# Splitting activation sums into high and low halves in the up projection instead of the down projection

## The chip, the cores and the metric

The kernel runs on one core of a Trainium2 chip. The metric is the device time of one execution in microseconds; the profile shows the same program executed once under the hardware profiler. Every time below is of that one core.

## What is computed

One layer of a hybrid decoder, followed by a final norm. This study touches its MLP alone:

```python
h2 = rmsnorm(x, norm2_g)
act = jnp.square(jax.nn.relu(jnp.einsum('bld,df->blf', h2, w_up)))
return x + jnp.einsum('blf,fd->bld', act, w_down)
```

There are 1024 tokens, a width of 1024 and a hidden width of 4096. All is float32.

## The kernel before

**Split products.** TensorE multiplies in float32r. Each operand is held as a high half and a low half: `split` (L73) casts the source to float32r on ACT (`nc.scalar.copy`, L77) and subtracts that from the source on DVE (L78). Every product is then three matmuls: high by high, high by low, low by high (L99 to L104, L715, L1091).

**Two projections.** The hidden width is cut into 32 rows of 128 (`NF`). The first four (`FS = 4`) are done in the standard way and stored in `act_dram`. The other 28 go in 14 pairs by a Strassen-Winograd scheme of seven products in place of eight.

**The up projection** (L984 to L1012) is a loop over these 14 pairs. In each pair `strassen_run` (L705) issues seven products of 12 matmuls, in the order 1, 5, 6, 2, 7, 3, 4. Products are summed in banks: `al_` takes 1, 6, 7 and 4, `be` takes 5 and 3, `ga` takes 2. Between them `keep_copy` (L718) copies a bank to a `cc` tile on ACT, and `put` (L987) adds bank and copy on DVE (L992) and applies ReLU on ACT (L993 or L990) into one half of one of the pair's two `go` tiles. The add after product 7 writes the half that holds a22. The tag `go` has two buffers, so the next pair's `go` tiles are the same two, and a write to them waits until all that reads the old contents is done, the DMAs too. After product 5 `up_load` loads the weights of a later pair (`strassen_load`, L683): two DMAs on SP into `raw` tiles of two buffers, sums of weight blocks on POOL (`s12`, L692 and L693; `s34`, L696 and L697), and splits (`hi`/`lo`, `sh`/`sl` twice, `eh`/`el`). The low half of `s34` is read by product 7 and product 3.

When a pair is complete its two tiles are squared (L998), four sums of blocks are made on DVE (L1006 to L1009), and seven blocks are written to `sum_dram` (L1012): a11, a21, a12 and a22 in the `go` tiles, and three in `sums`, a tile of one buffer. Each write is 128x512 float32, 256 KB, in rows of 512 bytes. It is issued from ACT's queue, but for the last pair from SP's.

**The down projection.** First come the four standard rows (L1021 to L1028, L1141 to L1144). Then the 28 rows go in seven groups `c` of two pairs, and each group in four units `m` of 256 tokens. A group's weights are loaded and split by `down_w` (L1044): loads on SP, block differences on POOL, splits on ACT and DVE. A unit's sums are loaded by `down_s` (L1068): one DMA of 896 KB on SP into `s_raw`, which has one buffer, then two splits: the five blocks of the first products into `s_hi` and `wide`, the two blocks of products 7 and 4 into a late tile (`lo` or `s_late`). A unit runs seven products of six matmuls (L1087). Their results are added to `x1` on DVE (L1097 to L1115); one of these adds, L1097, moves the bank `al` to `ga`, and the next product in `al` waits for it. Product 7 and product 4 of a unit are run inside the next unit.

**Order.** The source order is not the order in the queues. The tile framework gives every instruction its place by its own schedule, in which the source order is a priority, and sets the semaphores; each engine then runs its own queue strictly in order. Buffers are reused in turn per tag, and `reserve` (L669) lays out the tags of a pool.

Of the kernel before, what the change touches and what calls it, by code (L numbers as in the profile page):

```python
# [11 lines left out]
F32 = mybir.dt.float32  # L12
F32R = mybir.dt.float32r
# [5 lines left out]
P = 128  # L19
D = 1024  # L20
# [27 lines left out]
def hybrid_trunk_kernel(ctx: ExitStack, tc: tile.TileContext, x_tok, metas, vecs, gains, w_in, w_br, w_pool,  # L48
# [21 lines left out]
    def new(pl, shape, dt, tag, bufs=None):  # L70
        return pl.tile(shape, dt, tag=tag, name=nm(tag), **({} if bufs is None else {"bufs": bufs}))

    def split(hi, lo, src, eng=None, heng=None):  # L73
        if heng:
            heng.tensor_copy(hi, src)
        else:
            nc.scalar.copy(hi, src)  # L77
        (eng or nc.vector).tensor_sub(lo, src, hi.bitcast(F32))  # L78
# [58 lines left out]
    x1_dram = dram.tile([NB, P, D], F32, name="x1_dram")  # L137
    FS = 4
    act_dram = dram.tile([FS, P, T], F32, name="act_dram")
    sum_dram = dram.tile([(NF - FS) // 2, 4, P, 7, P], F32, name="sum_dram")  # L140


    hstack = ctx.enter_context(ExitStack())
# [525 lines left out]
    def reserve(pl, *tags):  # L669
        for tag, n, shape in tags:  # L670
            for _ in range(n):
                new(pl, [P, shape], F32, tag, n)
# [7 lines left out]
            t[w, i] = new(pl, [P, 4, 512], F32R, f"t{w}{i}")  # L680
        return [t["h", i] for i in range(4)], [t["l", i] for i in range(4)]

    def strassen_load(pl, src_a, src_b, eng=nc.gpsimd):  # L683
        ra = new(wst, [P, KD, P], F32, "raw")
        nc.sync.dma_start(ra, src_a)
        rb = new(wst, [P, KD, P], F32, "raw")
        nc.sync.dma_start(rb, src_b)
        ah, al = new(wst, [P, KD, P], F32R, "hi"), new(wst, [P, KD, P], F32R, "lo")
        split(ah, al, ra)
        s12, s34 = new(pl, [P, 2, 4, P], F32, "sf", 2), new(pl, [P, 2, 4, P], F32, "sf", 2)  # L690
        a11, a12, a21, a22 = ra[:, 0:4, :], ra[:, 4:8, :], rb[:, 0:4, :], rb[:, 4:8, :]
        eng.tensor_add(s12[:, 0], a21, a22)  # L692
        eng.tensor_sub(s12[:, 1], s12[:, 0], a11)  # L693
        s12h, s12l = new(pl, [P, 2, 4, P], F32R, "sh", 2), new(pl, [P, 2, 4, P], F32R, "sl", 2)
        split(s12h, s12l, s12)
        eng.tensor_sub(s34[:, 0], a11, a21)  # L696
        eng.tensor_sub(s34[:, 1], a12, s12[:, 1])  # L697
        s34h, s34l = new(pl, [P, 2, 4, P], F32R, "sh", 2), new(pl, [P, 2, 4, P], F32R, "sl", 2)
        split(s34h, s34l, s34)
        eh, el = new(pl, [P, 4, P], F32R, "eh", 2), new(pl, [P, 4, P], F32R, "el", 2)  # L700
        split(eh, el, a22)
        return {1: (ah[:, 0:4], al[:, 0:4]), 2: (ah[:, 4:8], al[:, 4:8]), 3: (s34h[:, 1], s34l[:, 1]), 4: (eh, el),
                5: (s12h[:, 0], s12l[:, 0]), 6: (s12h[:, 1], s12l[:, 1]), 7: (s34h[:, 0], s34l[:, 0])}
# [223 lines left out]
    with ExitStack() as st:  # L927
# [25 lines left out]
                nc.sync.dma_start(t, src)  # L953

        p2 = pool("up", 1, None, st)
        reserve(p2, ("go", 2, T), *STRASSEN_TAGS[1:])

        def up_load(f):
            if f < NF:
                return strassen_load(p2, w_up[f], w_up[f + 1], nc.gpsimd if f > FS + 2 else nc.vector)  # L960

        X1A = 4

# [20 lines left out]
        for f in range(FS, NF, 2):  # L984
            outs = [new(p2, [P, T], F32, "go", 2) for _ in range(2)]

            def put(r, c, ps, add):  # L987
                dst = outs[r][:, c * 512:(c + 1) * 512]
                if add is None:
                    nc.scalar.activation(dst, ps, AF.Relu)  # L990
                else:
                    nc.vector.tensor_add(dst, ps, add)  # L992
                    nc.scalar.activation(dst, dst, AF.Relu)  # L993

            lhs = strassen_run(p2, lhs, h2_hi, h2_lo, th, tl, put, lambda: up_load(f + 2),
                               first_rows if f + 2 == NF else None)
            for t in outs:
                nc.scalar.activation(t, t, AF.Square)  # L998
            (a11, a21), (a12, a22) = ((t[:, :512], t[:, 512:]) for t in outs)
            sums = new(p2, [P, 3, 512], F32, "sums", 1)  # L1000
            eng = nc.scalar
            if f + 2 == NF:
                eng = nc.sync
                x1 = new(dn, [P, NB, D], F32, "x1", 1)
                load_x1(range(X1A))
            nc.vector.tensor_sub(sums[:, 1], a11, a21)  # L1006
            nc.vector.tensor_add(a21, a21, a22)
            nc.vector.tensor_sub(sums[:, 0], a21, a11)
            nc.vector.tensor_sub(sums[:, 2], a12, sums[:, 0])  # L1009
            dst = sum_dram[(f - FS) // 2].rearrange("m p i t -> p i m t")  # L1010
            for i, t in enumerate((a11, a21, a12, sums[:, 0], sums[:, 2], sums[:, 1], a22)):
                eng.dma_start(dst[:, i], t.rearrange("p (m t) -> p m t", m=4))  # L1012

        load_x1(range(X1A, NB))
        st.close()
# [50 lines left out]
            return h, l  # L1066

        def down_s(c, m):  # L1068
            raw = new(dn, [P, 2 * D], F32, "s_raw", 1)[:, :14 * P].rearrange("p (u j) -> p u j", u=2)
            nc.sync.dma_start(raw, sum_dram[2 * c:2 * c + 2, m].rearrange("u p i t -> p u (i t)"))  # L1070
            h, l = new(dw, [P, 2, 5 * P], F32R, "s_hi", 2), new(dn, [P, 2 * D], F32R, "wide")
            l = l[:, :10 * P].rearrange("p (u t) -> p u t", u=2)
            split(h, l, raw[:, :, :5 * P])
            late = new(wst, [P, D], F32R, "lo") if (4 * c + m) % 3 else new(dn, [P, D], F32R, "s_late", 1)
            late = late.rearrange("p (v u t) -> p v u t", v=2, u=2)
            split(late[:, 0], late[:, 1], raw[:, :, 5 * P:])
            return (h, l), (late[:, 0], late[:, 1])

        class Unit:
            def __init__(self, tw, c, m):  # L1080
                self.tw, self.s, self.m = tw, down_s(c, m), m
                self.al, self.be, self.ga = (bank(t) for t in ("mm", "z", "tr"))

            def acc(self, r, c):
# [75 lines left out]
        prev, last = None, NU // 2 - 1  # L1160
        for c in range(NU // 2):
            tw = [down_w(2 * c), down_w(2 * c + 1)]
            if c == last:
                fg = new(wst, [P, D], F32, "hi")
                nc.sync.dma_start(fg, gains[2])
                wide = [new(dw, [P, 7 * 512], F32, ("wa", "wb")[c % 2]) for _ in range(3)]
                outs = [t[:, i * D:(i + 1) * D] for t in wide for i in range(3)]
            for m in range(4):
                unit = Unit(tw, c, m)
                if c == last and m == 3:  # L1170
                    unit.end(prev)
                    break
                unit.one()
                if prev:
                    prev.two()
                unit.three()
                if c == last:
                    final(m, 1)
                if prev:
                    prev.four()  # L1180
                    if c == last and m:
                        final(prev.m + 4, 0)
                prev = unit
# [60 lines left out]
```

## Time and profile before

| | us |
|---|---|
| Median of the three runs | 1981.67 |
| Their range | 1977.3 to 1984.02 |
| The profiled execution, its own time | 1980.0 |
| Its span, first to last instruction | 1978.2 |
| PE busy in the span | 1931.9 |
| DVE busy | 1291.9 |
| ACT busy | 844.0 |
| POOL busy | 329.1 |

PE is TensorE's matmul stream, PEld its weight loads, DVE is VectorE, ACT is ScalarE, POOL is GpSimd and SP is SyncE. An issue of a DMA from ACT's or SP's queue is written ACTq or SPq and is not counted as busy, though it takes its place in that queue. A line such as `sl<-sf,sh` names the tile written and the tiles read. Matmuls overlap: each is shown with its whole length, while the next one starts earlier. So PE shows as busy throughout when matmuls follow each other without a gap, and a stall shorter than the overlap is not seen as idle.

### The profile page before, as it was taken

To read this page: it belongs to the slowest core of one execution; us is meant where nothing else is said; L and a number is where in the kernel's file an instruction comes from. 1 tells how busy PE (TensorE), PEld (TensorE's weight loads), DVE (VectorE), ACT (ScalarE), POOL (GpSimd) and SP (SyncE) were. 2 spreads that over 40 slices of the span, in tenths; PEclk is the share of its full clock that TensorE was granted. 3 is DMA by queue.
4 is the path that set the end of the run, shared out by engine and by line. 5 is a ranking of instruction groups with operands and counts; after the bars stand their busy time and mean duration, and the time that the engine had idled before them with its cause. 6 is when DMAs were issued, how large, how long until landed. Compare 5 with 4: busy or idle time off the path is not lost.

```text
span 1978.2 us, 25779 instructions
## 1 busy us (share of the span) xinstructions
PE 1931.9 (98%) x9974; PEld 1647.4 (83%) x9974; DVE 1291.9 (65%) x1783; ACT 844.0 (43%) x1452; POOL 329.1 (17%) x280
## 2 busy tenths in 40 slices
PE   8999999999999999999999999999999999999998
PEld 7889899988899888888887888888888887777876
DVE  6677877666768844344334667479555546888887
ACT  6556654233324433333342112255544544343445
POOL 1000001111000033333320000000323212322322
PEclk9999999999999999999999999999999999999999
DMA  3000101110102233333326554242454557343433
GB/s 140 33 33 22 43 33 49 54 43 26 40 33 91 85 149 117 139 123 112 128 104 231 186 187 169 77 143 93 136 170 138 155 165 258 127 145 135 152 138 137
DMA packets 112076, 224.61 MB, mean 114 GB/s; under 512 B 8129, under 2 KB 58817, under 8 KB 111954
## 3 DMA queue, kind: packets, MB, share of 16 engines
q1 hardware_dynamic: 56706, 175.22, 25.9%
q10 hardware_dynamic: 55248, 47.75, 7.2%
q8 instruction: 78, 1.28, 0.3%
q14 instruction: 44, 0.36, 0.1%
HBM read 157.40 MB, written 65.54 MB: 113 GB/s over the span
## 4 chain that ended last, share of the span: by engine, by line
PE 76%; DVE 9%; issue 9%; DMA 3%; ACT 2%; POOL 1%; POOLq 0%; DVEq 0%; ACTq 0%; SPq 0%
PE mm L715 18%; PE mm L104 9%; PE mm L103 9%; PE mm L102 9%; PE z L715 9%; PE tr L715 5%; PE mm L1092 3%; PE z L1092 2%; PE av L362 1%; PE z L582 1%; DVE wb L78 1%; PE tr L1092 1%; DVE keep L339 1%; DVE wa L78 1%; DMA raw<-in_w_dn_dram 1%
## 5 line engine op out<-in xcount | busy, mean ns | idle before, releaser
L102 PE MATMUL mm<-h_hi,hi 128*128 128x384 f32 (+4 forms) x880 | 303.0, 345 | 1.4 <-DVE a L198 1.0
L103 PE MATMUL mm<-h_lo,hi 128*128 128x384 f32 (+4 forms) x880 | 295.2, 336 | 1.1 <-DVE h_lo L78 1.1
L104 PE MATMUL mm<-h_hi,lo 128*128 128x384 f32 (+4 forms) x880 | 295.8, 336 | 0.0
L103 PEld LDWEIGHTS mm<-h_lo,hi 128*128 128x128 f32 x880 | 166.6, 189 | 7.9 <-DVE h_lo L78 1.9
L104 PEld LDWEIGHTS mm<-h_hi,lo 128*128 128x128 f32 x880 | 166.0, 189 | 8.0
L102 PEld LDWEIGHTS mm<-h_hi,hi 128*128 128x128 f32 x880 | 166.0, 189 | 7.9 <-DVE a L198 1.4
L78 DVE TENSOR_TENSOR sl<-sf,sh 128x1024 fp32r<-128x1024 f32 x68 | 83.8, 1232 | 128.8 <-ACT sh L77 128.8
L692 POOL TENSOR_TENSOR sf<-raw 128x512 f32<-128x512 f32 x30 | 40.3, 1342 | 764.1 <-DMA raw<-in_w_up_dram 459.3
L78 DVE TENSOR_TENSOR lo<-raw,hi 128x1024 fp32r<-128x1024 f32 x76 | 95.7, 1259 | 45.2 <-ACT hi L77 44.8
L77 ACT CAST hi<-raw 128x1024 fp32r<-128x1024 f32 x76 | 79.9, 1052 | 77.0 <-PE mm L103 40.7
L715 PE MATMUL mm<-th,sh 128*128 128x512 f32 x272 | 106.2, 390 | 0.0
L77 ACT CAST sh<-sf 128x1024 fp32r<-128x1024 f32 x68 | 71.4, 1052 | 81.3 <-PE z L715 41.7
L715 PE MATMUL mm<-tl,sh 128*128 128x512 f32 x272 | 105.8, 389 | 0.0
L715 PE MATMUL mm<-th,sl 128*128 128x512 f32 x272 | 105.8, 389 | 0.0
L339 DVE TENSOR_TENSOR_SCAN keep<-keep 128x1040 f32<-128x1040 f32 (+3 forms) x64 | 88.9, 1390 | 25.7 <-ACT keep L332 18.9
L102 PE MATMUL mm<-b_hi,eh 128*128 128x512 f32 x256 | 99.6, 390 | 1.8 <-DVE mixed L884 1.8
L103 PE MATMUL mm<-b_lo,eh 128*128 128x512 f32 x256 | 100.1, 391 | 0.1
L104 PE MATMUL mm<-b_hi,el 128*128 128x512 f32 x256 | 99.6, 390 | 0.5 <-DVE el L78 0.5
L78 DVE TENSOR_TENSOR el<-raw,eh 128x512 fp32r<-128x512 f32 x34 | 36.2, 1064 | 64.5 <-ACT eh L77 61.3
L334 POOL TENSOR_SCALAR_AFFINE_SELECT keep<-keep 128x128 f32<-128x128 f32 x64 | 22.3, 348 | 300.2 <-ACT keep L332 260.2
L77 ACT CAST at_h<-tr 128x384 fp32r<-128x384 f32 (+2 forms) x112 | 54.5, 495 | 36.6 <-PE tr L349 34.9
L77 ACT CAST s_hi<-s_raw 128x1280 fp32r<-128x1280 f32 x28 | 35.4, 1266 | 80.9 <-DMA s_raw<-sum_dram 45.8
(439 smaller groups left out, 5019.2 us busy)
## 6 DMA issues: line engine op xcount, KB each, us to landing
raw<-in_w_in_dram SPq DMA_DIRECT2D x76, 512.0 KB, 3.7
s_raw<-sum_dram SPq DMA_DIRECT2D x28, 896.0 KB, 4.8
gate_dram<-go ACTq DMA_DIRECT2D x32, 512.0 KB, 2.6
go<-gate_dram SPq DMA_DIRECT2D x32, 512.0 KB, 3.7
raw<-in_w_up_dram SPq DMA_DIRECT2D x32, 512.0 KB, 3.8
raw<-in_w_dn_dram SPq DMA_DIRECT2D x29, 512.0 KB, 4.4
sum_dram<-go ACTq DMA_DIRECT2D x52, 256.0 KB, 4.7
sum_dram<-sums ACTq DMA_DIRECT2D x39, 256.0 KB, 4.8
```

The lines of the kernel that those rows point to most:

```text
L77: nc.scalar.copy(hi, src)
L78: (eng or nc.vector).tensor_sub(lo, src, hi.bitcast(F32))
L102: nc.tensor.matmul(ps, lh, rh, start=first, stop=False)
L103: nc.tensor.matmul(ps, lh, rl, start=False, stop=False)
L104: nc.tensor.matmul(ps, ll, rh, start=False, stop=last)
L334: nc.gpsimd.affine_select(out=t[:, :P], in_=t[:, :P], compare_op=ALU.is_gt, fill=1.0, base=0, pattern=[[1, P]], channel_multiplier=-1)
L339: nc.vector.tensor_tensor_scan(t, t, t, 1.0, op0=ALU.mult, op1=ALU.min)
L362: nc.tensor.matmul(av[:, :w], pair.vv[e][:, b, :], a[:, b, :w], start=i == 0 and a is at[0], stop=i == len(order) - 1 and a is at[1])
L582: nc.tensor.matmul(ps[:, c * 64:(c + 1) * 64], xc, low, start=True, stop=True)
L692: eng.tensor_add(s12[:, 0], a21, a22)
L715: nc.tensor.matmul(ps, lhs[i][x][:, k, :], rhs[i][y][:, k, :], start=fresh and k == 0 and n == 0, stop=k == 3 and n == 2, skip_group_check ...
L1092: nc.tensor.matmul(ps, x, y[:, rs], start=fresh and k == 0 and n == 0, stop=k == 1 and n == 2, skip_group_check=not fresh)
```

## The change

Four edits belong together.

- The up projection splits each of the seven blocks before it is written. The high half goes to a new tile `hs` of three buffers; the low half is written over the block itself. Both halves are written to `sum_dram`, which gets one more dimension `v` of two: 14 writes of 256 KB per pair in place of seven.
- The pool `up` reserves a list of tags with `hs` in it, and `strassen_load` in the up projection is called with `inplace=True`: `sf` has one buffer, and `s34` is written over `ra`, the `raw` tile that it is computed from.
- `down_s` loads high and low halves straight into the tiles that the matmuls read, in four DMAs per unit; `s_raw` and both splits go.
- `down_s` of the next unit is called right after a unit is made, one unit ahead of where it stood; `Unit` takes the loaded sums as an argument.

```diff
-    sum_dram = dram.tile([(NF - FS) // 2, 4, P, 7, P], F32, name="sum_dram")
+    sum_dram = dram.tile([(NF - FS) // 2, 4, 2, P, 7, P], F32, name="sum_dram")
...
-    def strassen_load(pl, src_a, src_b, eng=nc.gpsimd):
+    def strassen_load(pl, src_a, src_b, eng=nc.gpsimd, inplace=False):
...
-        s12, s34 = new(pl, [P, 2, 4, P], F32, "sf", 2), new(pl, [P, 2, 4, P], F32, "sf", 2)
+        s12 = new(pl, [P, 2, 4, P], F32, "sf", 1 if inplace else 2)
+        s34 = ra.rearrange("p (i k) c -> p i k c", i=2) if inplace else new(pl, [P, 2, 4, P], F32, "sf", 2)
...
-        reserve(p2, ("go", 2, T), *STRASSEN_TAGS[1:])
+        reserve(p2, ("go", 2, T), ("cc", 3, 512), ("sf", 1, D), *STRASSEN_TAGS[3:], ("hs", 3, 512))
...
-                return strassen_load(p2, w_up[f], w_up[f + 1], nc.gpsimd if f > FS + 2 else nc.vector)
+                return strassen_load(p2, w_up[f], w_up[f + 1], nc.gpsimd if f > FS + 2 else nc.vector, True)
...
-            dst = sum_dram[(f - FS) // 2].rearrange("m p i t -> p i m t")
+            dst = sum_dram[(f - FS) // 2].rearrange("m v p i t -> v p i m t")
             for i, t in enumerate((a11, a21, a12, sums[:, 0], sums[:, 2], sums[:, 1], a22)):
-                eng.dma_start(dst[:, i], t.rearrange("p (m t) -> p m t", m=4))
+                h, l = new(p2, [P, 512], F32R, "hs", 3), t.bitcast(F32R)
+                split(h, l, t)
+                for v, part in enumerate((h, l)):
+                    eng.dma_start(dst[v, :, i], part.bitcast(F32).rearrange("p (m t) -> p m t", m=4))
...
         def down_s(c, m):
-            raw = new(dn, [P, 2 * D], F32, "s_raw", 1)[:, :14 * P].rearrange("p (u j) -> p u j", u=2)
-            nc.sync.dma_start(raw, sum_dram[2 * c:2 * c + 2, m].rearrange("u p i t -> p u (i t)"))
             h, l = new(dw, [P, 2, 5 * P], F32R, "s_hi", 2), new(dn, [P, 2 * D], F32R, "wide")
             l = l[:, :10 * P].rearrange("p (u t) -> p u t", u=2)
-            split(h, l, raw[:, :, :5 * P])
             late = new(wst, [P, D], F32R, "lo") if (4 * c + m) % 3 else new(dn, [P, D], F32R, "s_late", 1)
             late = late.rearrange("p (v u t) -> p v u t", v=2, u=2)
-            split(late[:, 0], late[:, 1], raw[:, :, 5 * P:])
+            for v, main in enumerate((h, l)):
+                src = sum_dram[2 * c:2 * c + 2, m, v].rearrange("u p i t -> p u (i t)")
+                nc.sync.dma_start(main.bitcast(F32), src[:, :, :5 * P])
+                nc.sync.dma_start(late[:, v].bitcast(F32), src[:, :, 5 * P:])
             return (h, l), (late[:, 0], late[:, 1])
...
             tw = [down_w(2 * c), down_w(2 * c + 1)]
+            if not c:
+                s = down_s(0, 0)
...
             for m in range(4):
-                unit = Unit(tw, c, m)
+                unit, s = Unit(tw, s, m), None
+                if 4 * c + m + 1 < 4 * (last + 1):
+                    s = down_s(c + (m + 1) // 4, (m + 1) % 4)
```

More of the change, by code (lines that the diff above doesn't have):

```diff
@@ L1068, in down_s, with __init__ @@
         def down_s(c, m):
-            raw = new(dn, [P, 2 * D], F32, "s_raw", 1)[:, :14 * P].rearrange("p (u j) -> p u j", u=2)
-            nc.sync.dma_start(raw, sum_dram[2 * c:2 * c + 2, m].rearrange("u p i t -> p u (i t)"))
             h, l = new(dw, [P, 2, 5 * P], F32R, "s_hi", 2), new(dn, [P, 2 * D], F32R, "wide")
             l = l[:, :10 * P].rearrange("p (u t) -> p u t", u=2)
-            split(h, l, raw[:, :, :5 * P])
             late = new(wst, [P, D], F32R, "lo") if (4 * c + m) % 3 else new(dn, [P, D], F32R, "s_late", 1)
             late = late.rearrange("p (v u t) -> p v u t", v=2, u=2)
-            split(late[:, 0], late[:, 1], raw[:, :, 5 * P:])
+            for v, main in enumerate((h, l)):
+                src = sum_dram[2 * c:2 * c + 2, m, v].rearrange("u p i t -> p u (i t)")
+                nc.sync.dma_start(main.bitcast(F32), src[:, :, :5 * P])
+                nc.sync.dma_start(late[:, v].bitcast(F32), src[:, :, 5 * P:])
             return (h, l), (late[:, 0], late[:, 1])
         class Unit:
-            def __init__(self, tw, c, m):
-                self.tw, self.s, self.m = tw, down_s(c, m), m
+            def __init__(self, tw, s, m):
+                self.tw, self.s, self.m = tw, s, m
                 self.al, self.be, self.ga = (bank(t) for t in ("mm", "z", "tr"))
```

## The prediction

> **What bounds the kernel now.** I read the page's span first, then the busy time of each engine by stretch, then what TensorE (PE) waits for in the down projection, then one pair of the up projection in order of time. The windows' columns are: stretch, its length, busy time of PE, PEld, DVE, ACT and POOL, granted clock, DMA share, GB/s. The first row is the 14 Strassen pairs of the up projection, the second the turn to the down projection, the third its units up to the last, the fourth the tail, the fifth one pair.
>
> ```profile
> span 1978.2 us, 25779 instructions
> 1374.70:1641.20 266.50, 266.50 (x1177) 220.73 (x1177) 141.36 (x161) 134.89 (x185) 68.26 (x48) 1.00 0.52 151
> 1641.20:1686.50 45.30, 44.21 (x194) 35.91 (x193) 34.70 (x43) 15.81 (x19) 16.89 (x11) 1.00 0.68 245
> 1686.50:1955.50 269.00, 259.85 (x1124) 210.51 (x1123) 228.51 (x296) 115.09 (x161) 71.93 (x49) 0.99 0.42 144
> 1955.50:1978.20 22.70, 13.20 (x56) 9.92 (x54) 16.14 (x40) 11.23 (x29) 5.86 (x5) 0.89 0.31 116
> 1489.00:1508.05 19.05, 19.05 (x86) 15.78 (x85) 9.96 (x12) 9.54 (x13) 5.59 (x5) 1.00 0.54 153
> ```
>
> PE is busy without a gap in the up projection, so nothing can be gained there; work added to ACT or DVE is free only while PE never waits for it. In the units of the down projection PE is idle 269.00 - 259.85 = 9.15 us, and DVE is busy 228.51/269 = 85%: that is the only place where this change can gain. What PE waits for there (total, times, longest):
>
> ```profile
> PE mm L1092 <- DVE tr L1097: 7.7, 7, 2.3
> PE mm L1092 <- DVE wide L78: 1.3, 3, 0.5
> ```
>
> The second is the low half of the sums itself; the first is an add that stands in DVE's queue behind splits, those of the sums among them. One pair of the up projection, ACT's queue, then DVE's and PE's (start, length, engine):
>
> ```profile
> 1488.99 0.37 ACTq L1012 DMA_DIRECT2D sum_dram<-go  x1
> 1489.41 0.60 ACT L990 ACTIVATE go<-mm 128x512 f32<-128x512 f32 x1 [0.44 <-PE mm L715]
> 1490.96 1.06 ACT L998 ACTIVATE go<-go 128x1024 f32<-128x1024 f32 x1 [0.96 <-DVE sums L1006]
> 1491.93 0.56 ACT L720 COPY cc<-mm 128x512 f32<-128x512 f32 x1
> 1492.06 1.09 ACTq L1012 DMA_DIRECT2D sum_dram<-go  x2
> 1493.51 1.46 ACTq L1012 DMA_DIRECT2D sum_dram<-sums  x2
> 1495.01 1.50 ACTq L1012 DMA_DIRECT2D sum_dram<-go  x1
> 1496.84 0.59 ACT L720 COPY cc<-z 128x512 f32<-128x512 f32 x1 [4.35 <-DMA sum_dram<-go]
> 1497.33 0.62 ACT L77 CAST eh<-raw 128x512 fp32r<-128x512 f32 x1
> 1497.85 1.05 ACT L77 CAST sh<-sf 128x1024 fp32r<-128x1024 f32 x1
> 1498.79 0.59 ACT L720 COPY cc<-mm 128x512 f32<-128x512 f32 x1
> 1508.04 0.37 ACTq L1012 DMA_DIRECT2D sum_dram<-go  x1
> ```
> ```profile
> 1493.51 0.69 DVE L1009 TENSOR_TENSOR sums<-go,sums 128x512 f32<-128x512 f32 x1
> 1497.98 0.69 DVE L78 TENSOR_TENSOR el<-raw,eh 128x512 fp32r<-128x512 f32 x1 [3.78 <-ACT eh L77]
> 1498.93 1.23 DVE L78 TENSOR_TENSOR sl<-sf,sh 128x1024 fp32r<-128x1024 f32 x1 [0.26 <-ACT sh L77]
> 1502.78 0.69 DVE L992 TENSOR_TENSOR go<-mm,cc 128x512 f32<-128x512 f32 x1 [0.64 <-PE mm L715]
> ```
> ```profile
> 1499.86 0.39 PE L715 MATMUL mm<-th,sh 128*128 128x512 f32 x1
> 1500.32 0.39 PE L715 MATMUL mm<-th,sl 128*128 128x512 f32 x1
> 1502.58 0.39 PE L715 MATMUL z<-h_hi,sh 128*128 128x512 f32 x1
> ```
>
> Call 1488.99, the start of a pair's first product and of the last pair's spill, s. One product is 1502.58 - 1499.86 = 2.72 us; seven make the 19.05 us from spill to spill (1488.99 to 1508.04). Product 7, the fifth in the order 1, 5, 6, 2, 7, 3, 4, starts at s+10.87 and ends at s+13.59, product 4 starts at s+16.31. Two things are nearly late already. `sl`, the low half that product 7 reads in its third matmul (1500.32), is finished at 1498.93 + 1.23 = 1500.16: 0.16 us of room. And the add at 1502.78 (s+13.79) writes half of a `go` tile of which there are two; that half is free only when the last pair's a22 has landed.
>
> **Part 1, the up projection: 13 pairs that spill from ACT's queue.** Per pair the change adds 7 casts on ACT, 7 subtracts on DVE and 7 DMA issues on ACT's queue. The nearest rows: a 128x512 cast 0.62 (`eh`), its subtract 0.69 (`el`), an issue 0.37. DVE goes from 9.96 to 9.96 + 7 x 0.69 = 14.8 of 19.05: room. ACT goes from 9.54 busy + 7 x 0.37 issue = 12.1 to 9.54 + 7 x 0.62 + 14 x 0.37 = 19.1 of 19.05: its room is gone, and it must still wait for products in between.
>
> What sets the end is the `go` tile. Its a22 half is the last tile of the loop, so its low half leaves behind 13 other issues. On ACT between s and that issue stand relu 0.60, square 1.06, three copies 0.56 + 0.59 + 0.59, `eh` 0.62 and `sh` 1.05, which the products of this pair need in time: 5.07; then 7 casts, 4.34, and 13 issues, 4.81. That is 14.2. Casts that follow each other overlap (1497.33 to 1497.85 is 0.52 for one of 0.62); eight such places take off 0.8: 13.4. The landing:
>
> ```profile
> DMA to landing us min/median/max: 2.3/4.7/6.0
> sum_dram<-go ACTq DMA_DIRECT2D x52, 256.0 KB, 4.7
> raw<-in_w_up_dram SPq DMA_DIRECT2D x32, 512.0 KB, 3.8
> q10 hardware_dynamic: 48048, 23.86, 32.8%
> q1 hardware_dynamic: 3928, 14.32, 20.4%
> ```
>
> (The first and the last two are of the stretch 1393 to 1640; the first is the `go` tiles' DMAs, q10 is the spill.) With the median 4.7 the half is free at s+18.1 to s+18.9. The add waits from s+13.79 till then and takes 0.69; product 4 sums into the bank that the add reads and starts behind it, at s+18.8 to 19.6 in place of 16.31: 2.5 to 3.3 us of PE idle per pair, which come back in each pair because the next s moves by the same. Behind the waiting add DVE's whole queue stands, the next `sl` too. I take 3.0: 13 x 3.0 = **+39**. Below: if every write lands as the fastest, 2.3, the half is free at s+15.7 and the stall is 0.1: nothing. A gain is excluded, since PE has no idle time here. Above: three `hs` tiles serve seven casts, so casts four to seven each wait for a landing that ACT's order may not cover; two landings of 4.7 in a row (9.4) in front of the last tile instead of about 6.9 covered ones add 2.5: 5.5 per pair, +72.
>
> The sequencer's share of this is where the Trainium skill speaks the other way. In "DMA: Bandwidth & Descriptors", section "Issuing engines are not separate DMA queues", it holds that the time on the sequencer to start a DMA is usually small beside the DMA. By it the 7 added issues cost nothing, the half is free 2.6 us earlier, the stall is about 0.4, and the sum below would end near 1980. The rows agree on the single issue (0.37 beside 4.7) but put 14 of them into a queue that already holds 12.1 of 19.05 us, so I do not take it off.
>
> The DMA engines have room: the spill's 32.8% becomes 65.6%, with 20.4% of loads 86%. I price that at nothing; it can only lengthen landings, which the upper end holds.
>
> The in-place s34 keeps `raw` until `sl` is done: its reload moves from s+2.7 to s+11.2, lands 3.8 later at s+15.0, and cast 1.05 and subtract 1.23 end at s+17.3, before the next pair's first low half at s+19.5. Nothing, while the cover of 2.2 us holds. POOL then subtracts into `raw`, which the same finished split has read: nothing.
>
> **Part 2, the turn to the down projection.** The last pair's 7 spills go through SP; they become 14, behind seven splits and three `hs` tiles. Behind them on SP stand the loads of x1 and of the first down weights:
>
> ```profile
> 1652.87 0.69 SPq L1012 DMA_DIRECT2D sum_dram<-go  x1
> 1653.60 2.15 SPq L966 DMA_DIRECT2D x<-x_dram  x4
> 1655.79 0.43 SPq L1048 DMA_DIRECT2D raw<-in_w_dn_dram  x1
> ```
>
> Seven more tiles in threes are about two more landings, up to 8 us later for the weights. The standard rows cover part (PE idles only 1.09 us in this stretch, and 31 us lie between 1655.79 and the first unit at 1686.5): I take **+3**, between 0 and 8.
>
> **Part 3, the down projection.** What goes, 28 units (count, total, mean; the 512 wide pair has ten more of the same size under another tile name):
>
> ```profile
> L78 DVE TENSOR_TENSOR wide<-s_raw,s_hi 128x1280 fp32r<-128x1280 f32 x28 | 45.0, 1607 | 11.7 <-ACT s_hi L77 11.7
> L77 ACT CAST s_hi<-s_raw 128x1280 fp32r<-128x1280 f32 x28 | 35.4, 1266 | 80.9 <-DMA s_raw<-sum_dram 45.8 <-PE mm L1092 18.7 <-PE tr L1092 16.0
> L78 DVE TENSOR_TENSOR lo<-s_raw,lo 128x512 fp32r<-128x512 f32 x18 | 14.7, 818 | 0.0
> L77 ACT CAST lo<-s_raw 128x512 fp32r<-128x512 f32 x18 | 11.1, 616 | 0.0
> s_raw<-sum_dram SPq DMA_DIRECT2D x28, 896.0 KB, 4.8
> ```
>
> DVE loses 28 x (1.607 + 0.818) = 68 of its 228.5 us, ACT 28 x (1.266 + 0.616) = 53. On PE's path lie only the waits: the 1.3 behind `wide` goes whole, of the 7.7 behind L1097 most goes, since 2.4 us fewer stand in DVE's queue in each unit and the longest wait is 2.3. A stall also hides 0.16 us between PE's start spacing (0.23) and a matmul's length (0.39), so 9.15 idle in about a dozen places is 11. I take 8 of 11: **-8**; between -11 and 0. What is late next: the same add behind the weights' splits, which stay.
>
> Each unit now loads twice the bytes in four DMAs. Twice 4.8 is 9.6 us as an upper bound; from the last main product of unit m-1, which frees the buffers, to the first of unit m+1 lie 8 products of 1.36 (half of 2.72), 10.9. Hidden, by 1.3 us; without that cover see the third rival.
>
> **Sum** against the profiled execution's own 1980.0 us (span 1978.2, with 1.8 around it; 1.7 below the median 1981.67): 1980 + 39 + 3 - 8 = **2014**.
>
> **The rivals.** First, *faster: the spill hides*. It decides at a22's low half landing by s+15.6: issued by s+10.9 at 4.7, or by s+13.3 at 2.3. The issue order is the scheduler's, not the source's (the copy at 1491.93 stands ahead of four DMAs that precede it in the source), so it may put casts into ACT's gaps. Against it stands ACT's 19.1 of 19.05. Then only the gain is left: 1980 - 8 = 1972. A middle case, where 0.5 us per pair is left over, gives 1980 + 6 + 3 - 8 = 1981.
>
> Second, *product 7 binds before the tile*. `sl` has 0.16 us of room. If `eh`, `sh` stay behind the whole spill as they do now, 7 casts and 7 issues, 4.34 + 2.59 = 6.9, come ahead of them and product 7 is 6.8 late in each pair: +88, 1980 + 88 + 3 - 8 = 2063. For it: the order now. Against: the higher place of these loads in the source.
>
> Third, *the loads of the down projection bind*. If they miss the 10.9 by 2 us in each of 28 units, +56 on top, without the gain of 8: 1980 + 39 + 3 + 56 = 2078. Against: the 512 KB row at 3.8 and 896 KB at 4.8 say that bytes cost little, so twice is well under 9.6.
>
> **How the numbers follow.** Forecast 0.57, product 7 binding 0.20, hidden spill 0.10, middle 0.08, loads 0.05. The forecast's own range is 1980 + 0 + 0 - 11 = 1969 to 1980 + 72 + 8 = 2060, its bulk 1990 to 2045. For 8 in 10 over all: leave out the hidden spill and about 10% above, which gives 1981 to 2066. 0.3% (6 us) is what a measurement tells from no change; faster by more is the first rival and a little of the middle, 0.10; within it most of the middle, 0.07; slower 0.83.
>
> **What would show it.** Up projection: the window of a pair grows from 19.05 to about 22, PE gets idle time put down to `go` L992 or the DMAs of `sum_dram`, ACT's queue shows casts and issues back to back, DVE's L992 waits for a landing. If PE waits for `sl` or `sh` instead, it is the second rival; if the 13 pairs still take 247.6 us, the step from ACT's sum to the landing is wrong. Down projection: no casts or subtracts of sums, DVE near 160 of 269 us, PE idle 9.15 down to about 2; waits of PE for DMA of `sum_dram` would be the third rival.

## The result and the profile after

The changed kernel takes 2081.53 us (median of 4 runs, 2079.84 to 2083.18) beside 1981.08 us before (4 runs, 1977.3 to 1984.02): a ratio of 1.050, 95% interval 1.049 to 1.052. It is slower by 100 us. The direction was forecast, the size was not: 2081.53 lies above the range's end of 2066. One execution of the kernel called *up projection alone* below took 2217.5 us at a granted clock of 0.84, where its others had 0.98; it is left out of its median and ratio.

The windows of the changed kernel follow, cut at the first and last matmul of each stage: the up projection's pairs, the turn, the units, the tail, and one pair. The columns are those of the prediction's windows.

```profile
span 2081.4 us, 26154 instructions
1374.80:1746.00 371.20, 297.13 (x1177) 233.81 (x1175) 234.58 (x250) 184.27 (x275) 76.63 (x48) 0.89 0.59 170
1746.00:1803.40 57.40, 49.73 (x195) 38.77 (x194) 42.25 (x51) 19.20 (x27) 17.97 (x11) 0.91 0.84 292
1803.40:2072.70 269.30, 267.66 (x1177) 220.14 (x1175) 180.52 (x267) 76.58 (x127) 77.37 (x52) 1.00 0.70 236
2072.70:2081.40 8.70, 0.35 (x2) 0.00 (x0) 4.23 (x12) 3.38 (x10) 1.73 (x2) 0.71 0.32 121
1508.13:1535.59 27.46, 21.43 (x85) 16.75 (x84) 17.48 (x18) 13.43 (x21) 6.54 (x4) 0.88 0.59 171
```

Cut in the same way, the stages of the kernel before are 266.3, 45.5, 283.0 and 8.6 us. So the up projection loses 104.9, the turn 11.9, and the units gain 13.7: 104.9 + 11.9 - 13.7 = 103.1, of the 103.2 by which the profiled execution's own time grew (1980.0 to 2083.2). Two columns of the first row tell where to look: PE is idle for 371.2 - 297.1 = 74 us where it had no gap at all, and its granted clock is 0.89 where it was 1.00. A pair now takes 27.3 us in place of 19.04.

What waits in the up projection (stretch 1420 to 1640, the changed kernel; total, times, longest):

```profile
PE z L716 <- ACT sh L77: 47.4, 8, 6.1
ACT hs L77 <- DMA sum_dram<-go: 40.0, 6, 6.7
ACT sh L77 <- issue: 20.5, 8, 2.7
```

Once in each pair PE waits some 6 us, and for `sh`, not for a `go` tile. Here is one period in order of time, ACT's queue first (`...` stands for rows left out). The spill is what ACT does to square, cast and write a finished pair:

```profile
1508.13 0.60 ACT L991 ACTIVATE go<-mm 128x512 f32<-128x512 f32 x1 [1.45 <-PE mm L716]
1510.58 1.14 ACT L77 CAST hs<-go 128x512 fp32r<-128x512 f32 x2 [0.29 <-DVE go L1008]
1511.23 0.93 ACTq L1016 DMA_DIRECT2D sum_dram<-hs  x2
1515.68 2.67 ACTq L1016 DMA_DIRECT2D sum_dram<-go  x3
1518.39 1.14 ACT L77 CAST hs<-sums 128x512 fp32r<-128x512 f32 x2 [6.67 <-DMA sum_dram<-go]
...
1524.34 0.83 ACTq L1016 DMA_DIRECT2D sum_dram<-go  x1
1525.27 1.04 ACT L77 CAST sh<-sf 128x1024 fp32r<-128x1024 f32 x1 [2.57 <-issue]
...
1535.59 0.60 ACT L991 ACTIVATE go<-mm 128x512 f32<-128x512 f32 x1 [1.40 <-PE mm L716]
```
```profile
1519.95 0.39 PE L716 MATMUL tr<-h_hi,lo 128*128 128x512 f32 x1
1526.36 0.80 PE L716 MATMUL z<-th,sh 128*128 128x512 f32 x1 [6.03 <-ACT sh L77]
```
```profile
1511.78 1.63 POOL L694 TENSOR_TENSOR sf<-sf,raw 128x512 f32<-128x512 f32 x1
```

The spill begins with the ReLU at 1508.13; its last write is issued at 1524.34 to 1525.17. Right behind it stands the cast of s12 (`sh<-sf`). Its source was finished on POOL at 1511.78 + 1.63 = 1513.4, PE needed its result at 1520.2, and it starts at 1525.27: it had waited 11.9 us for its place in the queue. From the ReLU to that cast are 17.1 us, from the cast to the next spill's ReLU 10.3, together the period of 27.46. In those 10.3 us PE, freed by the cast, runs the products up to the last of the pair before, and ACT's ReLU waits for its end (1.40 us before 1535.59). So the pair is bound by a loop: the spill as one block in ACT's in-order queue, the cast behind it, the matmuls that wait for the cast, the next spill. Product 5 is the one that waits. The scheduler has moved products 7 and 4 of a pair into the next pair, so their operands are no longer the first that come too late. The row of 40.0 us names the landing of a `go` write. Before the cast at 1518.39 that landing came at 1517.96, just when DVE's third subtract ended (1513.88 + 4.08), and ACT's queue stood at the third write's issue until 1518.35; so no landing held up this cast.

Why the block is 17.1 us long, where from the ReLU to the first instruction behind the spill it was 1496.84 - 1489.41 = 7.4 before, the next rows show: DVE (changed kernel), then the groups of DVE from 1420 to 1640 in the changed kernel and in the kernel before.

```profile
1510.58 1.67 DVE L1009 TENSOR_TENSOR sums<-go 128x512 f32<-128x512 f32 x1
1512.29 1.67 DVE L1010 TENSOR_TENSOR sums<-go,sums 128x512 f32<-128x512 f32 x1
1513.88 4.08 DVE L78 TENSOR_TENSOR go<-go,hs 128x512 fp32r<-128x512 f32 x3
```
```profile
L78 DVE TENSOR_TENSOR go<-go,hs 128x512 fp32r<-128x512 f32 x32 | 39.1, 1261 | 0.0
L78 DVE TENSOR_TENSOR sums<-sums,hs 128x512 fp32r<-128x512 f32 x24 | 15.9, 690 | 18.2 <-ACT hs L77 18.2
```
```profile
L1006 DVE TENSOR_TENSOR sums<-go 128x512 f32<-128x512 f32 x11 | 15.9, 1446 | 4.4 <-ACT go L998 4.4
L1008 DVE TENSOR_TENSOR sums<-go 128x512 f32<-128x512 f32 x11 | 7.6, 692 | 0.4
L992 DVE TENSOR_TENSOR go<-mm,cc 128x512 f32<-128x512 f32 x12 | 8.3, 691 | 7.6 <-PE mm L715 7.6
```

The same subtract of 128x512 takes 0.69 us in one place and up to 1.77 in another. The long ones run while POOL makes the weight sums (1510.11 to 1516.8); the five in the rows above, four of them long, take 1.67 + 1.67 + 4.08 = 7.4 us in place of 5 x 0.69 = 3.45. ACT may issue the three `go` writes only behind them (1515.68 to 1518.35), and all that follows in its queue is 4 us late. An add of a bank and a copy has one input in PSUM and doesn't slow down: `L992 go<-mm,cc` of the kernel before ran beside POOL's sums in 10 of 12 cases and kept 0.69 in all, while `L1006`, with both inputs in SBUF, took 1.52 in the 10 of 11 cases beside POOL. The Trainium skill has this as a rule: in "SBUF — State Buffer", section "Who interferes with whom", a DVE instruction with both inputs in SBUF and a GpSimd instruction that reads SBUF share a port that one of them locks for its whole length, and a DVE instruction with one SBUF input, outside its two-port modes, isn't concerned. The traces agree (1.52 to 1.77 beside 0.69). It was to be seen before, too: the row of L1006 has 1446 ns where its neighbours have 692.

**The clock.** After the stall PE runs slow for a while: the matmuls from 1526.36 on start 0.43 us apart, those before 1519.95 0.227. The granted clock (the column before the DMA share) shows why, in three stretches of the changed kernel:

```profile
1522.50:1523.40 0.90, 0.00 (x0) 0.00 (x0) 0.90 (x2) 0.20 (x1) 0.00 (x0) 1.00 1.03 285
1523.60:1530.20 6.60, 3.84 (x9) 2.76 (x10) 2.43 (x3) 4.41 (x7) 0.00 (x0) 0.50 0.72 201
1530.40:1531.50 1.10, 1.10 (x6) 0.91 (x5) 0.69 (x1) 0.75 (x2) 0.00 (x0) 1.00 0.55 223
```

Counted over the starts of all 1,176 matmuls of the up projection in the changed kernel, 76.3 us of the 104.9 are stalls and some 27 are such slow spacing. In the 14 profiles of this study, from the first pair of the up projection to the end, the start of a matmul came late by 2.5 us or more (against the 0.227) at 88 places, and behind 84 of them six or more of the next 16 matmuls were slow; of 137 losses between 0.5 and 2 us 122 had three or fewer. "TensorE: Matmul & The Clock Gate" of the Trainium skill, section "What's actually happening", describes the slow state as one half of the clock, and lets it end after about 3.4 us of work; here the clock is back at 1530.3, 3.9 us after the first matmul. It also asks for about 3.4 us of idling before; here 22 of 25 losses between 2.5 and 3 us were enough, and 7 of 13 between 2 and 2.5.

In the clock records of the traces each slow stretch of the changed kernel's steady pairs lasts 6.83 us, and they come every 27.3 us; in *weight sums on DVE* and *blocks written twice* below they last 3.41 us and come every 23.9 us. These periods are eight and seven times 3.41 us. Whether a pair's time is drawn to a whole number of such steps, no run shows; a difference of one step between two kernels can in part be that.

### The profile page after: what moved, and what is told of

Its sections match the earlier page's. It is cut to its first block, busy times and chain, and to the rows that moved or that the text cites. A ratio compares the mean times of both kernels' runs of the same rounds, so it can differ in the third digit from the quotient of the medians.

```text
span 2081.4 us, 26154 instructions
## 1 busy us (share of the span) xinstructions
PE 1963.8 (94%) x9974; PEld 1664.5 (80%) x9974; DVE 1331.7 (64%) x1825; ACT 850.0 (41%) x1494; POOL 339.9 (16%) x280
## 4 chain that ended last, share of the span: by engine, by line
PE 71%; DVE 12%; issue 7%; ACT 5%; DMA 3%; ACTq 2%; POOL 1%; SPq 0%; DVEq 0%; POOLq 0%
PE mm L716 15%; PE mm L104 9%; PE mm L103 9%; PE mm L102 9%; PE mm L1096 7%; PE z L716 7%; PE z L1096 3%; PE tr L716 3%; ACTq L1016 2%; PE tr L1096 2%; PE av L362 2%; PE z L582 1%; DVE go L78 1%; DVE sums L78 1%; DVE sums L1010 1%
## 5 line engine op out<-in xcount | busy, mean ns | idle before, releaser
L693 POOL TENSOR_TENSOR sf<-raw 128x512 f32<-128x512 f32 x30 | 40.8, 1361 | 893.7 <-DMA raw<-in_w_up_dram 607.9
L78 DVE TENSOR_TENSOR sl<-sf,sh 128x1024 fp32r<-128x1024 f32 x54 | 66.6, 1234 | 157.7 <-ACT sh L77 157.7
L716 PE MATMUL z<-th,sh 128*128 128x512 f32 x136 | 57.5, 423 | 68.0 <-ACT sh L77 68.0
L716 PE MATMUL mm<-th,sh 128*128 128x512 f32 x272 | 115.3, 424 | 5.6 <-ACT cc L721 5.6
L716 PE MATMUL mm<-tl,sh 128*128 128x512 f32 x272 | 112.8, 415 | 0.0
L716 PE MATMUL mm<-th,sl 128*128 128x512 f32 x272 | 111.6, 410 | 0.0
L77 ACT CAST sh<-sf 128x1024 fp32r<-128x1024 f32 x54 | 56.7, 1051 | 94.3 <-PE mm L716 39.0
L716 PEld LDWEIGHTS z<-th,sh 128*128 128x128 f32 x136 | 26.6, 196 | 77.9 <-ACT sh L77 73.1
L716 PEld LDWEIGHTS mm<-th,sh 128*128 128x128 f32 x272 | 56.1, 206 | 23.9 <-ACT cc L721 12.2
L77 ACT CAST hs<-sums 128x512 fp32r<-128x512 f32 x42 | 24.8, 618 | 121.3 <-DMA sum_dram<-go 60.2
```

The lines of the kernel that those rows point to most:

```text
L716: nc.tensor.matmul(ps, lhs[i][x][:, k, :], rhs[i][y][:, k, :], start=fresh and k == 0 and n == 0, stop=k == 3 and n == 2, skip_group_check ...
```

## The experiments

Time is the median; the ratio of each experiment is against the kernel before on the same chip (1981.49 us for the first four experiments, 1983.45 for the next four, 1982.74 for the last four). The stages are from each one's profile.

| kernel | us | ratio, 95% | up | turn | units |
|---|---|---|---|---|---|
| before | 1981.08 | | 266.3 | 45.5 | 283.0 |
| after | 2081.53 | 1.050 (1.049 to 1.052) | 371.2 | 57.4 | 269.3 |
| in-place s34 alone | 1985.99 | 1.0015 (1.0006 to 1.0025) | 267.2 | 45.3 | 285.2 |
| down projection alone | 1965.72 | 0.992 (0.990 to 0.993) | 266.3 | 45.1 | 269.5 |
| up projection alone | 2094.38 | 1.057 (1.055 to 1.059) | 371.1 | 55.5 | 282.3 |
| spill from SP | 2037.24 | 1.027 (1.026 to 1.029) | 322.8 | 57.6 | 268.1 |
| high half only | 2006.07 | 1.012 (1.008 to 1.016) | 304.6 | 47.1 | 268.8 |
| blocks written twice | 2035.65 | 1.027 (1.023 to 1.030) | 327.6 | 53.2 | 268.7 |
| s12's cast on POOL | 2056.51 | 1.037 (1.033 to 1.042) | 346.4 | 55.4 | 268.2 |
| PE kept busy | 2081.46 | 1.050 (1.046 to 1.054) | 372.5 | 55.2 | 269.0 |
| weight sums on DVE | 2039.79 | 1.029 (1.027 to 1.031) | 330.1 | 54.9 | 268.1 |
| both: DVE sums, SP spill | 2015.20 | 1.016 (1.015 to 1.018) | 294.8 | 66.6 | 268.1 |
| two blocks split early | 1995.52 | 1.007 (1.005 to 1.008) | 277.8 | 52.7 | 278.1 |
| early call alone | 1989.75 | 1.0035 (1.0022 to 1.0047) | 266.3 | 45.2 | 292.8 |

The theory ("Theory Q" in the expectations): ACT's in-order queue binds each pair, with the spill as a block that holds up s12's cast, and POOL's sums lengthen the block through DVE. The rivals: the in-place s34 (with one `sf` buffer; rival I), the landing of the writes and the `go` tiles (rival G), and the slow clock. The cuts of code below show the lines that matter; `...` stands for lines left out.

### The parts of the change, each alone

The in-place s34, in the kernel before:

```diff
-        s12, s34 = new(pl, [P, 2, 4, P], F32, "sf", 2), new(pl, [P, 2, 4, P], F32, "sf", 2)
+        s12 = new(pl, [P, 2, 4, P], F32, "sf", 1 if inplace else 2)
+        s34 = ra.rearrange("p (i k) c -> p i k c", i=2) if inplace else new(pl, [P, 2, 4, P], F32, "sf", 2)
...
```

> The kernel before with one edit of the change alone: sf with one buffer, s34 written over raw, and the new list of reserved tags; the sums are spilled whole and split in the down projection as before. Theory Q (the stall is the cast of s12, queued on ACT behind the spill): about 1981 us, pairs of 19.04 us, PE without idle time in them. Rival I (the late reload of raw starves s12): the pairs grow to 22 us or more, 2020 us or above.

The down projection of the change, with the up projection of before:

```diff
-                eng.dma_start(dst[:, i], t.rearrange("p (m t) -> p m t", m=4))
+                eng.dma_start(dst[0, :, i], t.rearrange("p (m t) -> p m t", m=4))
...
+                src = sum_dram[2 * c:2 * c + 2, m, 0].rearrange("u p i t -> p u (i t)")
...
```

> The down projection of the change with the up projection of before: each block is written once, whole, and the down projection loads that same block as the high and as the low half (it leaves out the split of the sums altogether). If the 14 us that the units of the changed kernel gain come from the units alone, about 1967 us with units of 269 us; if the turn's 12 us belong to the down loads too, about 1979 us. If the gain hangs on the slower up projection, 1981 us.

The up projection of the change, with the down projection of before:

```diff
-            for v, main in enumerate((h, l)):
...
+            raw = new(dn, [P, 2 * D], F32, "s_raw", 1)[:, :14 * P].rearrange("p (u j) -> p u j", u=2)
+            nc.sync.dma_start(raw, sum_dram[2 * c:2 * c + 2, m, 0].rearrange("u p i t -> p u (i t)"))
+            split(h, l, raw[:, :, :5 * P])
...
```

> The up projection of the change with the down projection of before: both halves are written, the down projection loads the high half alone and splits it (the low half is left out of the result). Theory Q: pairs of 27.3 us, and with the turn's 12 us 1981 + 105 + 12 = 2098 us; if the turn's cost lies in the down loads, 2086 us.

The in-place s34 costs 1 us of the 105 in the up projection: it is not the cause. The down projection alone gives the whole gain of the units (269.5), the up projection alone the whole loss of the pairs (371.1) and most of that of the turn (55.5). So the change falls into two independent parts, and the turn belongs to the spill.

### Taking load off the spill

The spill's issues from SP's queue:

```diff
-            eng = nc.scalar
+            eng = nc.sync
```

> The changed kernel with all 14 writes of a pair issued from SP in place of ACT. Theory Q: ACT holds seven casts and no issue, the cast of s12 comes 5 us or more earlier and the pair falls from 27.3 to 22 us or less, 2010 us or below. Rival I: no change, 2081 us. Rival G (the forecast, a go tile is free only when the last block has landed): PE still waits, but for the adds at L993 behind landings of sum_dram, pairs of 20 to 22 us.

The low halves made, but not written:

```diff
-                for v, part in enumerate((h, l)):
+                for v, part in enumerate((h,)):
...
```

> The changed kernel with the low halves not written (the down projection loads the high half in their place, so the low halves are missing from the result): seven casts, seven subtracts and seven issues per pair. Theory Q: ACT's spill gets shorter by seven issues and by the waits for the subtracts between them, 27.3 to about 21 us per pair, 2000 us. If the casts and the three hs tiles make the stall, it stays near 27 us, 2075 us.

No splits, and each block written twice:

```diff
-                h, l = new(p2, [P, 512], F32R, "hs", 3), t.bitcast(F32R)
-                split(h, l, t)
-                for v, part in enumerate((h, l)):
+                for v in range(2):
...
```

> The changed kernel without the splits: each whole block is written twice, by 14 issues per pair (the split of the sums is left out). Theory Q, by ACT's queue alone: 14 issues and no cast make about as long a spill as seven casts and seven issues, so a pair between 20 and 23 us, 1995 to 2030 us. If only the casts count, 19.04 us and 1967 us.

The first pair of rows is the wait of PE in the kernel that spills from SP, the second in the one that writes each block twice (1420 to 1640):

```profile
PE mm L716 <- ACT cc L721: 22.9, 9, 3.5
DVE go L993 <- DMA sum_dram<-go: 4.5, 5, 1.8
```
```profile
PE z L716 <- ACT cc L721: 24.1, 9, 3.0
DVE go L993 <- DMA sum_dram<-go: 14.8, 10, 3.7
```

Each load taken off helps by much: the up projection falls by 48 us with the issues on another queue, by 67 without the seven low writes, by 44 without any cast or subtract. None comes back to 266. Theory Q had expected 2010, 2000 and at most 2030 us; all three came out slower (2037, 2006 and 2036), and in each PE has a next wait. With the same writes issued from another queue the kernel is 44 us faster: an issue also holds its place in an in-order queue until its data is made. By the sentence of the Trainium skill that the prediction weighed ("DMA: Bandwidth & Descriptors", "Issuing engines are not separate DMA queues": the sequencer's time for a start is usually small) the issues would have cost nothing. Writing fourteen blocks from ACT's queue, with no split at all, still costs 327.6 - 266.3 = 61 us; their issues take 0.86 us each there (median from 1420 to 1640), not 0.37. And each time PE still waits for ACT, now for the copies of the banks (`cc`), which stand behind what is left of the spill. The wait that the prediction had named, of `L993` on the landing of a `go` block, appears in the kernel that writes each block twice (14.8 us in ten adds), but on DVE and not as the reason that PE's wait names.

### The cast that PE waits for, and the clock

s12's cast on POOL, so that it does not stand in ACT's queue:

```diff
-        split(s12h, s12l, s12)
+        split(s12h, s12l, s12, None, nc.gpsimd if inplace else None)
```

> The changed kernel with one cast, that of s12, moved from ACT to POOL, all of the spill as it is. Theory Q: product 5 no longer waits behind the spill; PE then waits for the next thing behind it, s34's cast or the copies of the banks, and the pair falls by some 2 to 5 us, 2015 to 2055 us. If the length of the spill bounds the pair in another way (go tiles, hs tiles, landings), no change: 2081 us.

Twenty-four extra matmuls per pair, into a bank that nobody reads, so that PE does not idle:

```diff
+        if warm_up and tail is None:
+            w = bank("av")
+            for k in range(WARM):
+                nc.tensor.matmul(w, hi[:, k % 8, :P], hi[:, k % 8, :512], start=True, stop=True)
...
```

> The changed kernel with 24 matmuls of 512 columns into an unused bank in each pair, at the place where PE waits (5.4 us of work that nothing reads). If matmuls take 0.43 in place of 0.23 us after a stall because PE stood still, they now run at full rate and the pair falls from 27.3 to about 25.3 us, 2055 us, though PE has more to do. If the slow matmuls have another cause (operands, the memory's load), 27.3 us or more, 2081 us or above.

With the cast on POOL (1420 to 1640):

```profile
PE mm L716 <- ACT cc L721: 23.7, 8, 4.8
```

PE no longer waits for `sh` at all; the waits for `cc` have taken its place, and most pairs take 24 to 27 us: 25 of 105 us are won. So that cast was what PE met first, and the queue behind it is the bound.

The window 1420 to 1640 of the kernel with the extra matmuls:

```profile
1420.00:1640.00 220.00, 209.74 (x905) 169.60 (x904) 139.55 (x145) 106.02 (x163) 51.61 (x32) 0.99 0.60 172
```

PE is busy for 209.7 of 220 us and its clock is back at 0.99, and yet a pair takes 27.6 us and the kernel 2081 us. The expectation of a gain was wrong. The run does not part the clock from the rest, though. From s12's cast to the next ReLU, where the slow matmuls lay, the time is now 8.5 to 10.1 us, where it was 10.2. But ACT's block grew from 17.1 us to some 18 (ReLU at 1533.65, s12's cast at 1551.57), with ACT's queue in another order; why it grew isn't shown. So the long period needs no slow clock, and what the slow clock costs by itself stays open.

### POOL's sums and DVE

```diff
-                return strassen_load(p2, w_up[f], w_up[f + 1], nc.gpsimd if f > FS + 2 else nc.vector, True)
+                return strassen_load(p2, w_up[f], w_up[f + 1], nc.vector, True)
```

> The changed kernel with the sums of the weight blocks on DVE in place of POOL for all pairs; the order of PE's products is the same as in the changed kernel. Theory Q with the length of the spill as the price: in the changed kernel four DVE instructions of the spill take 1.67 to 1.77 us in place of 0.69 while POOL adds. Without POOL they take 0.69, the spill shortens by about 4 us, the pair falls from 27.3 to about 23.5 us: 2030 us. If ACT's own 14 issues and casts fill the spill, or if the four sums more on DVE (2.8 us per pair) delay the subtracts as much, no change: 2081 us.

The same edit, and the spill's issues from SP:

> The run before this one and the issue from SP together: sums of weight blocks on DVE, all 14 writes from SP. Theory Q: both delays of the spill are gone from ACT's queue, the pair falls below the 24 us that SP alone gave, to 20 to 22 us, 1985 to 2010 us. If the three hs tiles bound the casts then, 24 us, 2035 us.

In the first of the two, DVE gets four more instructions per pair, and its long ones become short:

```profile
L78 DVE TENSOR_TENSOR go<-go,hs 128x512 fp32r<-128x512 f32 x36 | 23.2, 685 | 0.3 <-ACT hs L77 0.2
L693 DVE TENSOR_TENSOR sf<-raw 128x512 f32<-128x512 f32 x9 | 6.2, 684 | 0.0
```

The subtract of a `go` block is 0.685 us where it was 1.261 on average, and the pair falls from 27.3 to 23.9 us, close to the 4 us read off the trace above; the block from the ReLU to s12's cast falls from 17.1 to 13.8 us. It is 41 us of the 105 in the up projection, from giving DVE *more* work: this shows POOL's contention as a cause. DVE does a sum in 0.68, for which POOL took 1.5 to 1.7.

In the second, the up projection is at 294.8. PE's waits have changed their reason (1420 to 1640):

```profile
PE mm L716 <- DVE go L993: 11.6, 8, 2.4
DVE go L993 <- DMA sum_dram<-go: 9.8, 10, 1.4
```

Now, with ACT's queue relieved and DVE's operations short, PE does wait for `L993`, and `L993` for the landing of `go` blocks: the forecast's mechanism, with a pair at 21 to 24 us, is among the *next* bounds. It is not alone: in the same stretch ACT's casts wait 17.7 us for `hs` tiles to land and DVE 18.1 us for `sums`, and no run parts the three. The turn grows to 66.6 us; in it PE waits once for 8.7 us for an add into `x1` (L1032), the wait that is followed under part 2 below. The kernel stays 1.6% slower than before, at 2015 us where 2010 at most was expected.

### Less of the change

Only the two blocks of products 7 and 4 split early, one `hs` buffer, nine writes per pair:

```diff
+                parts = [t]
+                if i > 4:
+                    parts = [new(p2, [P, 512], F32R, "hs", 1), t.bitcast(F32R)]
+                    split(*parts, t)
+                for v, part in enumerate(parts):
...
```

> The kernel before with a part of the change: only the two blocks that products 7 and 4 read (a11 - a21 and a22) are split in the up projection and written as both halves, nine writes per pair, hs with one buffer, nothing in place; the five others stay whole, are loaded into s_raw and split as before; down_s one unit ahead. Theory Q: ACT has room for two casts and two issues (2 us) in a pair, so pairs stay at 19.04 us; the units lose a third of the splits (0.8 of 2.4 us on DVE) and gain 3 to 7 us: 1974 to 1980 us. If any added spill stalls PE, 1990 us or more.

The call of `down_s` one unit ahead, in the kernel before:

```diff
+                unit, s = Unit(tw, s, m), None
+                if 4 * c + m + 1 < 4 * (last + 1):
+                    s = down_s(c + (m + 1) // 4, (m + 1) % 4)
...
```

> The kernel before with one edit of the change: down_s is called one unit ahead. s_raw has one buffer and the splits stay, so if the 14 us of the units come from DVE's relief, no change: 1981 us within 4. If they come from the earlier call, 1967 us.

Both missed. Two blocks of seven already cost 11.5 us in the up projection (20 us a pair) and 7.2 in the turn, and give 4.9 in the units. The early call alone costs 9.8 us in the units. The first row is the kernel with the early call, the second the changed kernel, in the units:

```profile
PE mm L1092 <- DVE tr L1097: 14.3, 7, 3.8
```
```profile
PE mm L1096 <- DVE tr L1101: 0.8, 1, 0.8
```

Called a unit ahead, the splits of the next unit's sums stand right before this unit's add in DVE's queue (in five of the six stalls over 0.3 us), and PE's wait for that add doubles from 7.7 to 14.3 us. In the changed kernel, without these splits, it falls to 0.8. The earlier call alone therefore doesn't give the units' gain; the splits must leave DVE. Whether the earlier call then adds to it was not run. No kernel that does the whole computation came out faster than the one before; only the down projection alone, which leaves the splits of the sums out altogether, was (1965.72 us).

## Why the prediction was wrong

**What bounds the kernel: right.** PE had no room in the up projection, and only the units could gain.

**Part 1, +39, measured +104.9: the step that failed is "What sets the end is the `go` tile".** In the changed kernel `L993` waited for a landing only once between 1420 and 1640, for 0.8 us; the writes landed in 2.7 us (`go`, `hs`), not 4.7. What set the period was the loop through ACT's queue, which the sentence before had filled to "19.1 of 19.05": the block of the spill, 17.1 us where it had been 7.4, held up s12's cast by 11.9 us, and PE stood 6 us in each pair for it. The prediction used ACT's number as one term in the way to a tile. It placed `eh` and `sh` ahead of the last write, as casts "which the products of this pair need in time", and did not ask which instruction of the next pair stands behind the block. The second rival did ask, and its kind is what happened: PE waits for `sh`, `eh`/`sh` stay behind the whole spill. It had product 7 for product 5, and +6.8 a pair for +8.3, and it got 0.20. The third rival's 2078 is nearer than its 2063, but by luck: PE waited for no load of the down projection.

Two terms were missing in both.
- *A subtract at 0.69* was the price of `el`, which runs while POOL is still. The subtracts of `go` blocks run beside POOL's sums and take up to 1.77. The weight sums on DVE put this at 41 us. The row of L1006 (1446 ns) in the kernel before was the warning; the prediction priced by line and size, and not by what else ran at that time.
- *The clock.* A stall of 6 us brings some 9 matmuls at half speed, some 27 us in all by the spacing. They lie in the loop, but how much they add is open: in the run with the clock restored ACT's block grew, and the time was the same.

**In-place s34, nothing: right** (1 us).

**Part 2, +3, measured +11.9.** The delay was of the kind that was named, only longer: the first weights' load came 11.6 us later, not "up to 8 us". The step that failed is the cover, "31 us lie between 1655.79 and the first unit". Here are the same loads in SP's queue of the changed kernel, and the waits from 1744 to 1806:

```profile
1768.76 0.65 SPq L1016 DMA_DIRECT2D sum_dram<-go  x1
1769.46 2.67 SPq L967 DMA_DIRECT2D x<-x_dram  x4
1772.18 0.44 SPq L1052 DMA_DIRECT2D raw<-in_w_dn_dram  x1
```
```profile
ACT hs L77 <- DMA sum_dram<-hs: 11.7, 3, 9.9
ACT wb L77 <- DMA raw<-in_w_dn_dram: 9.7, 2, 9.1
DVE wb L78 <- ACT wb L77: 4.2, 1, 4.2
PE av L102 <- DVE x L1032: 5.1, 1, 5.1
```

From the last matmul of the up projection to the weights' load are 1772.18 - 1746.0 = 26.2 us, before 1655.79 - 1641.2 = 14.6. The row of `ACT hs` is the three `hs` tiles: the last pair's casts wait for them to land. PE reaches the first unit without a wait in both kernels, 0.23 us after the start of the last matmul of the standard rows. It waits earlier, in the standard rows, for an add into `x1` (`L1032`); that add stands in DVE's queue behind splits of the first down weights (`wb`), whose casts wait for the late load. So the delay reached PE before the first unit, through DVE's in-order queue, where a distance of 31 us is no cover. By the spacing of starts the turn holds 7.7 us of stalls and 5.8 of slow matmuls, before 1.1 and 0.6, and 7.7 + 5.8 - 1.7 = 11.8.

**Part 3, -8, measured -13.7: mechanism right, size too small.** DVE fell from 240.4 us in the units to 180.5, 60 of the 68 forecast. PE's idle time, cut in the same way, fell from 283.0 - 272.6 = 10.4 us to 269.3 - 267.66 = 1.6, near the forecast of 2. But the bound of 11 took only stalls into account that the windows show as idle. By the spacing of starts, the units before lost 11.9 us in stalls and 4.0 in slow matmuls behind them, after 2.1 and 0.6: 15.9 - 2.7 = 13.2. The loads of the doubled bytes stayed hidden, as forecast; PE waited for none. One reading was loose: in six of the seven waits for L1097 before, a split of weights (`wa` or `wb`) is the last split ahead of that add, and only once does a split of the sums end within 2.5 us before the stall; so it is DVE's queue as a whole that got shorter.

**The chances.** The range reached 2066 because the case of product 7 was to be taken in with its 2063. Its price held 7 casts and 7 issues, and no waits inside the block. With half of the 4 us by which POOL lengthens the block it would be 1980 + 13 x 8.8 + 3 - 8 = 2089, with all of them 2115: an estimate after the fact, above the 2081.53 that were measured, so the parts of that price don't fit either.

## What to carry to other kernels

When a change lengthens the block that an engine's in-order queue holds for one round, find the instruction of the *next* round that stands behind the block, and who waits for it; that wait, not a tile's landing at the far end, came first here. Price an operation by a row that ran beside the same other engines: a mean of 1446 ns among rows of 692 is a contention, and work added to that place pays it too. The distance from a load to the stage that it is for is no cover while other work stands behind the load's casts and splits in some engine's queue; follow the delay through those queues.

## What was not expected of the hardware

- VectorE takes 0.69 us for a 128x512 float32 subtract, and up to 1.77 beside GpSimd's sums, which themselves go from 1.29 (`L693` before) to 1.6 us; an add with one input in PSUM keeps 0.69 beside them. Moving those sums onto the busier VectorE made the kernel 2% faster than the changed one.
- TensorE's matmuls start 0.43 us apart in place of 0.227, at a granted clock of 0.50, after losses from about 2.5 us on (84 of 88), and few of them after most losses between 0.5 and 2 us (122 of 137).
- An issue on ACT's queue is 0.37 us by its median from 1420 to 1640, before and after, but single ones take up to 1.59 and 1.53; where the 14 of a pair have no cast of a block between them (*blocks written twice*) the median is 0.86.
